# A hybrid decoder block: the two output projections change places, and each head pair's convolution is woven into that pair's own substitution

## The chip, the cores and the metric

One core of one Trainium2 chip. The metric is the device time of one execution in microseconds (us). The chip's engines run side by side, each through its own instructions in a fixed order: TensorE (PE in the profile; PEld are its weight loads), VectorE (DVE), ScalarE (ACT), GpSimd (POOL), and SyncE (SP), which here only issues transfers.

## The reference, cut to what matters

One decoder block on 528 positions (16 learned ones, then 512) of 1024 channels. Two token mixers read the same normalised input `h`, their outputs are projected, gated and added, and a projection, a norm and a gated feed-forward part follow:

```python
p = h @ w_in
y_conv = swish(LN(causal_dwconv31(glu(p)))) @ w_conv_out      # conformer branch
y_rwkv = (LN_head(recurrence(r, decay, k, v, a, b)) + bonus) * g @ w_rwkv_out   # 16 heads of 64
y = sigmoid(gA) * y_conv + sigmoid(gB) * y_rwkv
h = LN(alpha * h + y @ w_o)
h = LN(alpha * h + conv_gated_mlp(h))
```

The recurrence runs over positions, S_t = S_{t-1} diag(w_t) + (S_{t-1} a_t) b_t^T + v_t k_t^T. The kernel solves it in 9 chunks of 64 positions: within a chunk a triangular system is inverted, and the state goes from chunk to chunk.

## The kernel before, in words

Everything lies with channels on the 128 partitions and positions along the free axis. A product of float32 data is made from three products of float32r parts: `wload` (L155) and `wsplit` (L143, with `split`, L136) load a 512 KB block of weights into `wr` (two buffers), round it on ScalarE (`wh`, L138) and take the rest on VectorE (`wl`, L141); `gemm` (L158) then issues 3 x 8 matmuls for a half of the positions (258 or 256 columns). A projection of one 128-channel block is two halves, 48 matmuls.

The 16 heads are done as 8 pairs. The steps of a pair `p`, each one letter in the string `SCHEDULE`:

- `K` (`rkv`, L339): three projections for k, v, r.
- `P` (`prep`, L347): decays (a scan, L383), the arrays `AR`, `BK`, `BT`, `UV`, and the chunk matrices `Gt` (L452). `AR`, `Gt`, `BT`, `UV` have two buffers, so `P` of pair p overwrites what `C` of pair p-2 has read.
- `S` (`solve`, L482): the blocks of `Gt` go through DRAM (`dA`, L493) into a layout `L` (L502), where VectorE inverts all triangles by 31 dependent steps (L520, L524, L526) and, for the short first chunk, 15 more (L530). The result goes to DRAM (`dT`, L544). A second digit names a convolution whose VectorE instructions are put between the dependent steps; the function `behind` fixes that order: each step of the substitution stands behind the instruction taken from the convolution.
- `C` (`merge`, L548, and `chain`, L581): fetches the inverse, combines blocks by matmuls (L566, L571), then goes through the 9 chunks one after the other on TensorE and ScalarE (L584, L603, L606, L620), with a state update on VectorE (L615).
- `F` (`finish`, L624): head norm, the gate by `g_up`, and the store of the pair's output to DRAM (`o_dr`, L673).
- `G` (`glu`, L678): two projections and the gated input of the convolution for block p. `conv` (L701) is the 31-tap convolution of the block, 48 VectorE instructions (L711, L712, L714, L722), stored to `c_dr` (L725).
- `T`: a convolution by itself at lowest priority (`back`). `A`: one of 16 gate projections (`gate`, L728), stored to `g_dr`. `N`: `conv_norm` (L745), the layer norm over the convolution's 1024 channels: sums, subtractions, squares, a reciprocal, then swish, rounding and rest (L755 to L783).

The string gives priorities, not times. The compiler's scheduler keeps one order per engine; instructions traced under `front` go ahead of others, a ready instruction of low priority fills a gap, and the blocks of weights stream through `wr`, `wh`, `wl` in the order of the string. In the kernel before, block 0 and block 5 are convolved by themselves (`T0`, `T5`), and the other blocks are woven into the substitution of the pair before theirs (`S01`, `S12`, `S23`, `S34`, `S56`, `S67`); `S4` and `S7` carry none.

After the string come, in this order, the conformer projection (L811 to L821, weights `w_conv_out`, input `zh`, `zl` from `conv_norm`, result to `ya_dr`), the recurrence's projection (L830 to L855, weights `w_rwkv_out`, input `oh`, `ol`, which are loaded from `o_dr` (L834) and split; it adds `ya` and leaves `yh`, `yl`), and `w_o` with the first layer norm in two halves of positions (L862 to L897). Of the 8 blocks of `w_o`, `NKEEP` = 6 are loaded once and kept for both halves, 2 are loaded for each half. The feed-forward part follows.

SBUF pools are opened on a left and a right stack; a tile of a new pool waits for the tiles that lay at its address. `scan` (left) holds what `P`, `S`, `C`, `F` share, `proj` (right) the rest of them and the convolutions.

Of the kernel before, what the change touches and what calls it, by code (L numbers as in the profile page):

```python
# [11 lines left out]
F32 = mybir.dt.float32  # L12
F32R = mybir.dt.float32r
AF = mybir.ActivationFunctionType
ALU = mybir.AluOpType
# [3 lines left out]
P = 128  # L19
D = 1024  # L20
NK = D // P
# [11 lines left out]
NQ = T - Q0  # L33
# [9 lines left out]
GN_EPS = 64e-5  # L43
EXPM05 = float(np.exp(-0.5))
BACK = 3000
NKEEP = 6
GW = 132


SCHEDULE = ("G0 K0 P0 T0 G1 S01 K1 P1 C0 K2 F0 G2 S12 K3 P2 C1 G3 F1 K4 S23 G4 P3 C2 F2 A S34 K5 P4 C3 F3 G5 S4 A "  # L50
            "T5 K6 P5 G6 C4 F4 S56 P6 C5 K7 F5 G7 S67 A A A P7 C6 F6 S7 A A C7 A A N A A A A A A A F7")


@with_exitstack
def hybrid_block(ctx: ExitStack, tc: tile.TileContext, a, out, dbg=None):
    nc = tc.nc
    V, S, G, TE = nc.vector, nc.scalar, nc.gpsimd, nc.tensor
# [5 lines left out]
    def pool(stack, name, side, **kw):  # L63
        return stack.enter_context(tc.tile_pool(name=name, bufs=1, side=side, reuse_waits="tile", **kw))

    front = tc.high_priority
# [18 lines left out]
    gbank = lambda: bank("g", 3)  # L85
# [50 lines left out]
    def split(dst_hi, dst_lo, src, hi_engine="s"):  # L136
        if hi_engine == "s":
            S.copy(out=dst_hi, in_=src)  # L138
        else:
            V.tensor_copy(out=dst_hi, in_=src)  # L140
        V.tensor_tensor(out=dst_lo, in0=src, in1=dst_hi.bitcast(F32), op=ALU.subtract)  # L141
# [13 lines left out]
    def wload(dram, c0, wpool=None, after=None, bufs=2):  # L155
        return wsplit(dram[:, c0:c0 + P].rearrange("(k p) n -> p k n", p=P), [P, NK, P], wpool, after, bufs)

    def gemm(ps, w, xh, xl, sl, nk=NK):  # L158
        wh, wl = w
        for k in range(nk):  # L160
            TE.matmul(ps, wh[:, k, :], xh(k, sl), start=(k == 0), stop=False)  # L161
            TE.matmul(ps, wl[:, k, :], xh(k, sl), start=False, stop=False)  # L162
            TE.matmul(ps, wh[:, k, :], xl(k, sl), start=False, stop=(k == nk - 1))  # L163
# [59 lines left out]
    with tc.tile_pool(name="start", bufs=1, side="right", reuse_waits="tile") as st:  # L223
        prow = [st.tile([P, P], F32, name=f"prow{i}") for i in range(6)]
        with front():
            xt = []
            for i in range(5):
                n = NMETA if i == 0 else P
# [18 lines left out]
        fw = a["ffn_dw"][0].rearrange("j (c p) -> (j c) p", p=P)  # L247
# [51 lines left out]
        for i, n in ((1, 112), (2, 128), (3, 120), (4, 88), (5, 44)):  # L299
# [15 lines left out]
                    in1=taps[:, :, 1, :], op=ALU.add)  # L315
# [470 lines left out]
    for step in SCHEDULE.split():  # L786
        what, p, q = step[0], int(step[1:2] or 0), int(step[2:] or -1)
        if what == "K":
            raw[p] = rkv(p)
        elif what == "P":  # L790
            prs[p] = prep(p, *raw.pop(p))
        elif what == "S":
            solved[p] = solve(prs[p], conv(q, cpads.pop(q)) if q >= 0 else ())
        elif what == "C":
            with front():
                merge(prs[p], *solved[p])
                ys[p] = chain(prs[p])
        elif what == "F":
            finish(prs[p], ys.pop(p))
        elif what == "G":  # L800
            cpads[p] = glu(p)
        elif what == "T":
            with back():
                for _ in conv(p, cpads.pop(p)):
                    pass
        elif what == "A":
            gate(gates.pop(0))
        elif what == "N":
            ctx_a1.close()
            rb, zh, zl = conv_norm()  # L810
    for j in range(NK):  # L811
        ga = rb.tile([P, NQ], F32, name="ga", bufs=2)
        nc.sync.dma_start(out=ga, in_=g_dr[j])
        w = wload(a["w_conv_out"][0], P * j)
        for sl, n in qsl:
            pt = gbank()
            gemm(pt[:, :n], w, lambda k, s: zh[k][:, s], lambda k, s: zl[k][:, s], sl)
            with front():
                V.scalar_tensor_tensor(out=ga[:, sl], in0=ga[:, sl], scalar=1.0, in1=pt[:, :n],
                                       op0=ALU.add, op1=ALU.mult)  # L820
        nc.sync.dma_start(out=ya_dr[j], in_=ga)  # L821
    ctx_b1.close()
    ctx_a2.close()


    ctx_b2, ctx_o = ExitStack(), ExitStack()
    op = pool(ctx_o, "rout", "left")
    mp = pool(ctx_b2, "mix", "right")
    ot = lambda dt, name: op.tile([P, NQ], dt, name=name, tag="ot", bufs=16)
    yt = lambda dt, name: mp.tile([P, NQ], dt, name=name, tag="yt", bufs=16)  # L830
    oh, ol, yh, yl = [], [], [], []
    for j in range(NK):
        o_t = op.tile([P, NQ], F32, name="o_t", bufs=2)
        nc.sync.dma_start(out=o_t, in_=o_dr[j])  # L834
        oh.append(ot(F32R, "oh"))
        ol.append(ot(F32R, "ol"))
        split(oh[j], ol[j], o_t)
    for j in range(NK):
        gb_ = op.tile([P, NQ], F32, name="gb_", bufs=2)
        nc.sync.dma_start(out=gb_, in_=g_dr[8 + j])  # L840
        ya = op.tile([P, NQ], F32, name="ya", bufs=2)
        nc.sync.dma_start(out=ya, in_=ya_dr[j])
        w = wload(a["w_rwkv_out"][0], P * j)
        yh.append(yt(F32R, "yh"))
        yl.append(yt(F32R, "yl"))
        for sl, n in qsl:
            pt = gbank()
            gemm(pt[:, :n], w, lambda k, s: oh[k][:, s], lambda k, s: ol[k][:, s], sl)
            with front():
                V.scalar_tensor_tensor(out=gb_[:, sl], in0=gb_[:, sl], scalar=1.0, in1=pt[:, :n],  # L850
                                       op0=ALU.add, op1=ALU.mult)
            V.tensor_tensor(out=ya[:, sl], in0=ya[:, sl], in1=gb_[:, sl], op=ALU.add)
            S.activation(out=yh[j][:, sl], in_=ya[:, sl], func=AF.Copy, scale=0.5)
            V.scalar_tensor_tensor(out=yl[j][:, sl], in0=ya[:, sl], scalar=0.5, in1=yh[j][:, sl].bitcast(F32),
                                   op0=ALU.mult, op1=ALU.subtract)  # L855


    ctx_o.close()
    h1h, h1l = hhi[:, :, Q0:T], hlo[:, :, Q0:T]
    ctx_f = ExitStack()  # L860
    fw = pool(ctx_f, "upw", "left")
    kept = [wload(a["w_o"][0], P * j, mp, bufs=NKEEP) for j in range(NKEEP)]  # L862
    half_tile = lambda name, n, bufs: mp.tile([P, 258], F32, name=name, bufs=bufs)[:, :n]
    for (t0, t1), (sl, n) in zip(QH, qsl):
        pm, pv = abank(), abank()
        xs = []
        s1, s2 = half_tile("s1", n, 1), half_tile("s2", n, 1)
        for j in range(NK):
            w = kept[j] if j < NKEEP else wload(a["w_o"][0], P * j)
            pt = gbank()  # L870
            gemm(pt[:, :n], w, lambda k, s: yh[k][:, s], lambda k, s: yl[k][:, s], sl)
            x1 = half_tile("x1", n, 10)
            with front():
                V.scalar_tensor_tensor(out=x1, in0=hlo[:, j, t0:t1].bitcast(F32), scalar=ALPHA,
                                       in1=pt[:, :n], op0=ALU.mult, op1=ALU.add)
                V.scalar_tensor_tensor(out=x1, in0=hhi[:, j, t0:t1].bitcast(F32), scalar=ALPHA,
                                       in1=x1, op0=ALU.mult, op1=ALU.add)
            xs.append(x1)
            if j > 0:
                V.tensor_tensor(out=s1, in0=xs[0] if j == 1 else s1, in1=x1, op=ALU.add)  # L880
        TE.matmul(pm[:, :n], ones_d, s1, start=True, stop=True)
        with front():
            for j in range(NK):
                V.tensor_tensor(out=xs[j], in0=xs[j], in1=pm[:, :n], op=ALU.subtract)
                sq = s2 if j == 0 else half_tile("xsq", n, 2)
                S.activation(out=sq, in_=xs[j], func=AF.Square)
                if j > 0:
                    V.tensor_tensor(out=s2, in0=s2, in1=sq, op=ALU.add)
            TE.matmul(pv[:, :n], ones_d, s2, start=True, stop=True)
            rs1 = mp.tile([P, 258], F32, name="rs1")[:, :n]  # L890
            S.activation(out=rs1, in_=pv[:, :n], func=AF.Sqrt, bias=eps_ln)
            V.reciprocal(out=rs1, in_=rs1)
            for j in range(NK):
                V.tensor_tensor(out=xs[j], in0=xs[j], in1=rs1, op=ALU.mult)
                S.activation(out=xs[j], in_=xs[j], func=AF.Identity, scale=par("ln1_g", j), bias=par("ln1_b", j))
                split(h1h[:, j, sl], h1l[:, j, sl], xs[j], "s")
    dump("h1", h1h.bitcast(F32))  # L897


    fl = ExitStack()  # L900
    ctx_b2.close()
    fp = pool(fl, "ffn", "right")
    hidh = fp.tile([P, NF, SEQ], F32R, name="hidh")
# [113 lines left out]
```

## Time and profile before

| | us |
|---|---|
| runs | 1181.91, 1185.55, 1191.15 (median 1185.55) |
| the profiled execution, its own time | 1188.6 |
| its span | 1186.6 |
| TensorE busy (share of the span) | 1128.4 (95%) |
| VectorE busy | 870.5 (73%) |
| ScalarE busy | 560.5 (47%) |

The profile is one execution. The span is the time from the first to the last instruction that it records; 2.0 us of the execution's own time lie outside. An instruction's line is that of the kernel's file, of a helper's where a helper issues it. "Busy" of TensorE counts matmuls that overlap each other.

### The profile page before, as it was taken

Reading aid. Unit: us, or ns where it says so; the run is one execution under the profiler, and the core shown is the slowest. Engines: PE = TensorE matmul, PEld = TensorE weight load, DVE = VectorE, ACT = ScalarE, POOL = GpSimd, SP = SyncE. Lnnn points to the kernel's source line nnn. Section 1 sums busy time; section 2 is a strip of 40 time slices with the busy share of each in tenths; the row PEclk is TensorE's granted clock in tenths of the full one; section 3 lists DMA queues with packets and bytes.
Section 4 is the critical chain, followed back from the end, with each engine's and each line's share of the span. In section 5 each row is a group of like instructions: output and inputs, shape, how many; then the busy total and the mean of one; then the engine's idle time right before and its main releaser. Section 6 shows DMA issues by size and latency. Waiting matters only on the chain.

```text
span 1186.6 us, 22669 instructions
## 1 busy us (share of the span) xinstructions
PE 1128.4 (95%) x8718; PEld 1062.5 (90%) x8718; DVE 870.5 (73%) x2195; ACT 560.5 (47%) x1195; POOL 85.0 (7%) x242
## 2 busy tenths in 40 slices
PE   4998999999999999999978989999999999999997
PEld 3997989989898989998978989989999999998885
DVE  8598988989899998986495346688876666652227
ACT  3544355647556565666575433346433443432120
POOL 6001011101101110101000000000000000000000
PEclk9999999999999999999898989999999999999999
DMA  5324241333424143344443376523332323343321
GB/s 159 82 80 106 64 117 41 90 82 89 95 60 108 41 104 84 79 121 108 135 125 85 103 209 193 164 58 85 107 100 80 104 75 107 90 134 98 93 85 71
DMA packets 202439, 118.99 MB, mean 100 GB/s; under 512 B 50036, under 2 KB 186397, under 8 KB 202331
## 3 DMA queue, kind: packets, MB, share of 16 engines
q1 hardware_dynamic: 182992, 113.81, 34.1%
q10 hardware_dynamic: 17515, 3.17, 1.5%
q8 instruction: 68, 1.11, 0.4%
q0 software_dynamic: 1824, 0.57, 0.2%
q14 instruction: 40, 0.33, 0.1%
HBM read 102.24 MB, written 15.28 MB: 99 GB/s over the span
## 4 chain that ended last, share of the span: by engine, by line
PE 60%; DVE 8%; DMA 7%; ACT 3%; issue 2%; ACTq 0%; SPq 0%; DVEq 0%; POOL 0%; POOLq 0%
PE ps_g L161 13%; PE ps_g L162 13%; PE ps_g L163 13%; PE ps_x L584 7%; PE psf L961 3%; PE psf L963 3%; PE psf L962 3%; DMA wr<-in_w_o_dram 2%; DMA t22s<-dT 1%; DMA o_t<-o_dr 1%; DVE wl L141 1%; ACT wh L138 1%; PE ps_a L450 1%; DMA wr<-in_ffn_up_dram 1%; PE ps_m L571 1%
## 5 line engine op out<-in xcount | busy, mean ns | idle before, releaser
L161 PE MATMUL ps_g<-hhi,wh 128*128 128x256 f32 (+2 forms) x1648 | 477.2, 290 | 7.9 <-ACT hf_t L277 3.9
L162 PE MATMUL ps_g<-hhi,wl 128*128 128x256 f32 (+2 forms) x1648 | 477.3, 290 | 0.0
L163 PE MATMUL ps_g<-hlo,wh 128*128 128x256 f32 (+2 forms) x1648 | 474.6, 289 | 0.0
L161 PEld LDWEIGHTS ps_g<-hhi,wh 128*128 128x128 f32 x1648 | 312.8, 190 | 11.3 <-ACT hf_t L277 4.5
L162 PEld LDWEIGHTS ps_g<-hhi,wl 128*128 128x128 f32 x1648 | 312.4, 190 | 2.6 <-issue 0.6
L163 PEld LDWEIGHTS ps_g<-hlo,wh 128*128 128x128 f32 x1648 | 312.9, 190 | 1.3 <-issue 0.4
L141 DVE TENSOR_TENSOR wl<-wr,wh 128x1024 fp32r<-128x1024 f32 x151 | 184.1, 1220 | 96.6 <-ACT wh L138 96.0
L138 ACT CAST wh<-wr 128x1024 fp32r<-128x1024 f32 x151 | 158.0, 1047 | 124.8 <-PE psf L962 75.2
L722 DVE SCALAR_TENSOR_TENSOR cev<-cd,drv,cev 128x257 f32<-128x257 f32 x216 | 99.1, 478 | 0.1
L919 ACT COPY pu<-ps_g 128x258 f32<-128x258 f32 (+1 forms) x88 | 32.8, 373 | 111.1 <-PE ps_g L163 111.0
L584 PE MATMUL ps_x<-UV,Gt 128*66 128x64 f32 (+1 forms) x576 | 71.3, 246 | 4.2 <-DMA Gt<-dT 3.8
L584 PEld LDWEIGHTS ps_x<-UV,Gt 128*66 128x66 f32 (+1 forms) x576 | 65.5, 168 | 6.1 <-DMA Gt<-dT 4.0
L961 PE MATMUL psf<-wh,hidh 128*128 128x512 f32 x176 | 69.3, 394 | 0.0
L963 PE MATMUL psf<-wl,hidh 128*128 128x512 f32 x176 | 69.0, 392 | 0.0
L962 PE MATMUL psf<-wh,hidl 128*128 128x512 f32 x176 | 68.3, 388 | 0.0
L926 DVE SCALAR_TENSOR_TENSOR u<-pu,prm,u 128x512 f32<-128x512 f32 x88 | 65.7, 748 | 1.3
L714 DVE SCALAR_TENSOR_TENSOR csh<-cpad,drv,csh 128x257 f32<-128x257 f32 x120 | 57.5, 479 | 0.5
L615 DVE SCALAR_TENSOR_TENSOR Sb<-Sb,lc,ps_x 64x64 f32<-64x64 f32 x112 | 31.3, 280 | 32.7 <-PE ps_x L584 31.2
L924 DVE TENSOR_SCALAR u<-pu,prm 128x512 f32<-128x512 f32 x44 | 21.2, 485 | 43.5 <-ACT pu L919 43.4
L524 DVE TENSOR_TENSOR stmp<-L,W 128x60 f32<-128x60 f32 (+21 forms) x216 | 45.3, 210 | 1.3
L526 DVE TENSOR_TENSOR W<-W,stmp 128x60 f32<-128x60 f32 (+21 forms) x216 | 45.2, 209 | 1.0
L161 PE MATMUL ps_g<-zh,wh 128*128 128x258 f32 (+1 forms) x128 | 38.5, 303 | 7.6 <-ACT zh L138 7.6
(308 smaller groups left out, 1991.9 us busy)
## 6 DMA issues: line engine op xcount, KB each, us to landing
wr<-in_w_in_dram SPq DMA_DIRECT2D x59, 512.0 KB, 4.3
wr<-in_ffn_up_dram SPq DMA_DIRECT2D x44, 512.0 KB, 4.0
wr<-in_ffn_down_dram SPq DMA_DIRECT2D x22, 512.0 KB, 3.7
wr<-in_w_o_dram SPq DMA_DIRECT2D x10, 512.0 KB, 4.9
g_dr<-gt SPq DMA_DIRECT2D x16, 257.0 KB, 3.0
L<-dA SPq DMA_DIRECT2D x32, 128.0 KB, 4.2
wr<-in_w_conv_out_dram SPq DMA_DIRECT2D x8, 512.0 KB, 4.4
wr<-in_w_rwkv_out_dram SPq DMA_DIRECT2D x8, 512.0 KB, 5.6
```

The costliest lines, as they stand in the source:

```text
L138: S.copy(out=dst_hi, in_=src)
L141: V.tensor_tensor(out=dst_lo, in0=src, in1=dst_hi.bitcast(F32), op=ALU.subtract)
L161: TE.matmul(ps, wh[:, k, :], xh(k, sl), start=(k == 0), stop=False)
L162: TE.matmul(ps, wl[:, k, :], xh(k, sl), start=False, stop=False)
L163: TE.matmul(ps, wh[:, k, :], xl(k, sl), start=False, stop=(k == nk - 1))
L584: mm = lambda o, l, r, start: TE.matmul(o, l, r, start=start, stop=True, skip_group_check=True)
L714: yield V.scalar_tensor_tensor(out=cs_, in0=x1[:, i:i + NM], scalar=dcol(D_SCW, 8 * i + j) if i < HT else dcol(D_HCW, 8 * 2 * i + j), in1= ...
L722: yield V.scalar_tensor_tensor(out=yp[:, b, :] if lasttap else ev[:, b, :], in0=d[:, i:i + NM], scalar=dcol(D_HCW, 8 * (2 * i + b) + j), i ...
L926: V.scalar_tensor_tensor(out=u, in0=p_[:, t:t + SEQ], scalar=pcol(C_FW, 44 * t + m), in1=u, op0=ALU.mult, op1=ALU.add)
L961: TE.matmul(acc[t][d], hidh[:, k, ts], wd[k][0][:, ds], start=(k == 0), stop=False)
L962: TE.matmul(acc[t][d], hidl[:, k, ts], wd[k][0][:, ds], start=False, stop=False)
L963: TE.matmul(acc[t][d], hidh[:, k, ts], wd[k][1][:, ds], start=False, stop=(k == NF - 1))
```

## The change

The two projections change places. The outputs of the pairs are loaded, all eight into buffers of their own, and projected first; that result times its gate goes to `ya_dr`. `conv_norm` is traced after that projection and no longer has a letter in the string. The conformer's projection comes second, reads `ya` back, adds, and leaves `yh`, `yl`. Each convolution is woven into the substitution of its own pair (`S00`, `S11`, to `S77`); no `T` is left. The string places the gate projections anew: of 16, one each stands before `K5`, `K6` and `S66`, 2 before `S77`, 1 before `C7`, 7 before `F7` and 3 behind it. `NKEEP` is 4, so 4 blocks of `w_o` are loaded for each half. The pool `mix` moves to the left stack, and the small tiles of the first layer norm get a pool `norm1` on the right.

```diff
-NKEEP = 6
+NKEEP = 4
-SCHEDULE = ("G0 K0 P0 T0 G1 S01 K1 P1 C0 K2 F0 G2 S12 K3 P2 C1 G3 F1 K4 S23 G4 P3 C2 F2 A S34 K5 P4 C3 F3 G5 S4 A "
-            "T5 K6 P5 G6 C4 F4 S56 P6 C5 K7 F5 G7 S67 A A A P7 C6 F6 S7 A A C7 A A N A A A A A A A F7")
+SCHEDULE = ("G0 K0 P0 S00 K1 G1 P1 C0 K2 F0 S11 K3 P2 C1 G2 F1 K4 S22 P3 C2 G3 F2 A K5 S33 P4 C3 G4 F3 A K6 S44 P5 C4 "
+            "G5 F4 K7 S55 P6 C5 G6 F5 A S66 P7 C6 G7 F6 A A S77 A C7 A A A A A A A F7 A A A")
...
-        elif what == "N":
-            ctx_a1.close()
-            rb, zh, zl = conv_norm()
+
+    ctx_a2.close()
+    ctx_o = ExitStack()
+    op = pool(ctx_o, "rout", "left")
+    ot = lambda dt, name: op.tile([P, NQ], dt, name=name, tag="ot", bufs=16)
+    oh, ol = [], []
     for j in range(NK):
+        o_t = op.tile([P, NQ], F32, name="o_t", bufs=NK)
+        nc.sync.dma_start(out=o_t, in_=o_dr[j])
+        oh.append(ot(F32R, "oh"))
+        ol.append(ot(F32R, "ol"))
+        split(oh[j], ol[j], o_t)
+    for j in range(NK):
+        gb_ = op.tile([P, NQ], F32, name="gb_", bufs=2)
+        nc.sync.dma_start(out=gb_, in_=g_dr[8 + j])
+        w = wload(a["w_rwkv_out"][0], P * j)
+        for sl, n in qsl:
+            pt = gbank()
+            gemm(pt[:, :n], w, lambda k, s: oh[k][:, s], lambda k, s: ol[k][:, s], sl)
+            with front():
+                V.scalar_tensor_tensor(out=gb_[:, sl], in0=gb_[:, sl], scalar=1.0, in1=pt[:, :n],
+                                       op0=ALU.add, op1=ALU.mult)
+        nc.sync.dma_start(out=ya_dr[j], in_=gb_)
+    ctx_a1.close()
+    rb, zh, zl = conv_norm()
+    ctx_o.close()
+    ctx_f, ctx_b2 = ExitStack(), ExitStack()
+    fw = pool(ctx_f, "upw", "left")
+    mp = pool(ctx_b2, "mix", "left")
...
+        ya = mp.tile([P, NQ], F32, name="ya", bufs=2)
+        nc.sync.dma_start(out=ya, in_=ya_dr[j])
         w = wload(a["w_conv_out"][0], P * j)
+        yh.append(yt(F32R, "yh"))
+        yl.append(yt(F32R, "yl"))
         for sl, n in qsl:
             pt = gbank()
             gemm(pt[:, :n], w, lambda k, s: zh[k][:, s], lambda k, s: zl[k][:, s], sl)
...
-        nc.sync.dma_start(out=ya_dr[j], in_=ga)
...
-            V.tensor_tensor(out=ya[:, sl], in0=ya[:, sl], in1=gb_[:, sl], op=ALU.add)
+            V.tensor_tensor(out=ya[:, sl], in0=ya[:, sl], in1=ga[:, sl], op=ALU.add)
             S.activation(out=yh[j][:, sl], in_=ya[:, sl], func=AF.Copy, scale=0.5)
...
+    ctx_n = ExitStack()
+    lnp = pool(ctx_n, "norm1", "right")
     kept = [wload(a["w_o"][0], P * j, mp, bufs=NKEEP) for j in range(NKEEP)]
-    half_tile = lambda name, n, bufs: mp.tile([P, 258], F32, name=name, bufs=bufs)[:, :n]
+    half_tile = lambda name, n, bufs: lnp.tile([P, 258], F32, name=name, bufs=bufs)[:, :n]
```

## Rows read from the trace of the kernel before

**Rows 1.** The page's part 1: busy us, share of the span, instructions.
```profile
PE 1128.4 (95%) x8718; PEld 1062.5 (90%) x8718; DVE 870.5 (73%) x2195; ACT 560.5 (47%) x1195; POOL 85.0 (7%) x242
```

**Rows 2.** Busy time by stretch: length, PE (matmuls), PEld, DVE, ACT, POOL, clock, DMA, GB/s.
```profile
560.00:580.00 20.00, 18.05 (x135) 16.46 (x134) 8.09 (x28) 11.51 (x33) 2.05 (x4) 0.83 0.28 57
...
600.00:620.00 20.00, 15.78 (x126) 14.73 (x125) 19.17 (x56) 17.49 (x37) 1.72 (x2) 0.99 0.39 121
620.00:640.00 20.00, 13.61 (x84) 13.11 (x85) 15.05 (x37) 12.07 (x21) 0.00 (x0) 0.67 0.19 37
...
680.00:700.00 20.00, 16.99 (x135) 16.16 (x134) 8.34 (x13) 6.06 (x8) 0.00 (x0) 0.96 0.88 250
700.00:720.00 20.00, 19.56 (x141) 19.11 (x141) 11.08 (x24) 7.03 (x12) 0.00 (x0) 0.87 0.58 180
...
820.00:840.00 20.00, 20.00 (x172) 20.00 (x171) 17.59 (x25) 11.94 (x19) 0.00 (x0) 1.00 0.38 107
```

**Rows 3.** Waits of PE: line, releaser, us in total, times, longest.
```profile
PE ps_g L161 <- ACT zh L138: 7.6, 1, 7.6
...
PE ps_g L161 <- ACT oh L138: 2.9, 3, 1.5
```

**Rows 4.** Busy time by stretch, three longer ones (columns as in rows 2).
```profile
160.00:500.00 340.00, 334.00 (x2749) 310.32 (x2749) 306.34 (x1000) 202.99 (x509) 44.24 (x119) 0.99 0.34 81
540.00:600.00 60.00, 57.89 (x466) 53.89 (x465) 34.26 (x124) 35.62 (x91) 5.56 (x15) 0.94 0.51 133
...
588.00:631.00 43.00, 32.26 (x243) 30.29 (x243) 41.24 (x125) 31.88 (x63) 1.72 (x2) 0.87 0.34 111
```

**Rows 5.** By stretch, L722 alone (31 per convolution), then tile W alone: DVE busy.
```profile
0.00:161.00 161.00, 28.58 (x62) 0.99 0.36 101
...
437.00:501.00 64.00, 16.78 (x37) 1.00 0.38 89
...
588.00:632.00 44.00, 12.59 (x58) 0.00 (x0) 0.86 0.34 108
```

**Rows 6.** Timeline of SP's queue: start, us, issued transfers.
```profile
437.31 1.25 SPq L544 DMA_DIRECT2D dT<-W  x2
...
501.36 1.21 SPq L544 DMA_DIRECT2D dT<-W  x2
...
547.64 1.21 SPq L544 DMA_DIRECT2D dT<-W  x2
...
631.18 1.21 SPq L544 DMA_DIRECT2D dT<-W  x2
...
677.75 0.38 SPq L673 DMA_DIRECT2D o_dr<-on  x1
...
700.32 2.57 SPq L834 DMA_DIRECT2D o_t<-o_dr  x2
```

**Rows 7.** Timeline of ACT, the last chunk of pair 7.
```profile
667.10 0.26 ACT L620 COPY Y<-ps_x 64x128 f32<-64x128 f32 x1 [0.75 <-PE ps_x L584]
```

**Rows 8.** Groups of DVE: busy us, mean ns of one, idle before them.
```profile
L141 DVE TENSOR_TENSOR wl<-wr,wh 128x1024 fp32r<-128x1024 f32 x151 | 184.1, 1220 | 96.6 <-ACT wh L138 96.0
L722 DVE SCALAR_TENSOR_TENSOR cev<-cd,drv,cev 128x257 f32<-128x257 f32 x216 | 99.1, 478 | 0.1
...
L714 DVE SCALAR_TENSOR_TENSOR csh<-cpad,drv,csh 128x257 f32<-128x257 f32 x120 | 57.5, 479 | 0.5
```

**Rows 9.** Tiles on, o_t (landing), oh, gt: ns min/median/max of one, first and last start.
```profile
DMA to landing us min/median/max: 3.0/3.0/3.6
...
DMA to landing us min/median/max: 3.9/5.1/6.2
...
L161 PE MATMUL ps_g<-oh,wh x128: 277/282/583, 693.7 to 747.1; 128*128 128x258 f32 x64, 128*128 128x256 f32 x64
...
L736 ACT ACTIVATE gt<-ps_g,drv x32: 461/476/480, 276.0 to 614.7; 128x258 f32<-128x258 f32 x16, 128x256 f32<-128x256 f32 x16
```

**Rows 10.** The page's part 6: transfers of w_o, KB each, us to landing.
```profile
wr<-in_w_o_dram SPq DMA_DIRECT2D x10, 512.0 KB, 4.9
```

More of the change, by code (lines that the diff above doesn't have):

```diff
@@ L807, in hybrid_block @@
             gate(gates.pop(0))
-        elif what == "N":
-            ctx_a1.close()
-            rb, zh, zl = conv_norm()
-    for j in range(NK):
[L812 to L820, printed above, removed]
-        nc.sync.dma_start(out=ya_dr[j], in_=ga)
[L822 to L833, printed above, removed]
+    ctx_a2.close()
[3 more added lines that the diff above has]
+    oh, ol = [], []
+    for j in range(NK):
+        o_t = op.tile([P, NQ], F32, name="o_t", bufs=NK)
         nc.sync.dma_start(out=o_t, in_=o_dr[j])
@@ L840, in hybrid_block @@
         nc.sync.dma_start(out=gb_, in_=g_dr[8 + j])
-        ya = op.tile([P, NQ], F32, name="ya", bufs=2)
-        nc.sync.dma_start(out=ya, in_=ya_dr[j])
         w = wload(a["w_rwkv_out"][0], P * j)
-        yh.append(yt(F32R, "yh"))
-        yl.append(yt(F32R, "yl"))
         for sl, n in qsl:
@@ L851, in hybrid_block @@
                                        op0=ALU.add, op1=ALU.mult)
-            V.tensor_tensor(out=ya[:, sl], in0=ya[:, sl], in1=gb_[:, sl], op=ALU.add)
+        nc.sync.dma_start(out=ya_dr[j], in_=gb_)
[5 more added lines that the diff above has]
+    mp = pool(ctx_b2, "mix", "left")
+    yt = lambda dt, name: mp.tile([P, NQ], dt, name=name, tag="yt", bufs=16)
+    yh, yl = [], []
+    for j in range(NK):
+        ga = mp.tile([P, NQ], F32, name="ga", bufs=2)
+        nc.sync.dma_start(out=ga, in_=g_dr[j])
+        ya = mp.tile([P, NQ], F32, name="ya", bufs=2)
+        nc.sync.dma_start(out=ya, in_=ya_dr[j])
+        w = wload(a["w_conv_out"][0], P * j)
+        yh.append(yt(F32R, "yh"))
+        yl.append(yt(F32R, "yl"))
+        for sl, n in qsl:
+            pt = gbank()
+            gemm(pt[:, :n], w, lambda k, s: zh[k][:, s], lambda k, s: zl[k][:, s], sl)
+            with front():
+                V.scalar_tensor_tensor(out=ga[:, sl], in0=ga[:, sl], scalar=1.0, in1=pt[:, :n],
+                                       op0=ALU.add, op1=ALU.mult)
+            V.tensor_tensor(out=ya[:, sl], in0=ya[:, sl], in1=ga[:, sl], op=ALU.add)
             S.activation(out=yh[j][:, sl], in_=ya[:, sl], func=AF.Copy, scale=0.5)
@@ L855, in hybrid_block @@
                                    op0=ALU.mult, op1=ALU.subtract)
-    ctx_o.close()
+    ctx_b1.close()
     h1h, h1l = hhi[:, :, Q0:T], hlo[:, :, Q0:T]
-    ctx_f = ExitStack()
-    fw = pool(ctx_f, "upw", "left")
+    ctx_n = ExitStack()
+    lnp = pool(ctx_n, "norm1", "right")
     kept = [wload(a["w_o"][0], P * j, mp, bufs=NKEEP) for j in range(NKEEP)]
-    half_tile = lambda name, n, bufs: mp.tile([P, 258], F32, name=name, bufs=bufs)[:, :n]
+    half_tile = lambda name, n, bufs: lnp.tile([P, 258], F32, name=name, bufs=bufs)[:, :n]
     for (t0, t1), (sl, n) in zip(QH, qsl):
@@ L889, in hybrid_block @@
             TE.matmul(pv[:, :n], ones_d, s2, start=True, stop=True)
-            rs1 = mp.tile([P, 258], F32, name="rs1")[:, :n]
+            rs1 = lnp.tile([P, 258], F32, name="rs1")[:, :n]
             S.activation(out=rs1, in_=pv[:, :n], func=AF.Sqrt, bias=eps_ln)
@@ L900, in hybrid_block @@
     fl = ExitStack()
+    ctx_n.close()
     ctx_b2.close()
```

## The prediction

> **What bounds the kernel now.** I read the page's busy shares first, then busy time by stretch, then the waits of TensorE, then the queue of transfers for the times at which each pair's steps end. TensorE is busy 1128.4 of 1186.6 us [rows 1], so it bounds nearly everything, and what a change can win lies in the few stretches where it is not dense. The reader is to compare the counts of matmuls: a dense stretch of 20 us holds 172 (the last of [rows 2]). The five sparse ones around the end of the head pairs hold 135, 126, 84, 135 and 141 [rows 2], short of dense by 37 + 46 + 88 + 37 + 31 = 239 matmuls; at 20/172 = 0.1163 us each that is 27.8 us. The waits say why. Near 620 TensorE stands 7.6 us for the first `zh`, that is for the norm over the convolutions, and near 690 for `oh`, the outputs of the pairs [rows 3]. In both places the clock drops (granted 0.67 and 0.87 of full speed on average, so part of the stretch ran at 1.2 instead of 2.4 GHz after TensorE had stood idle) [rows 2].
>
> By busy time the same five stretches lack only 2.0 + 4.2 + 6.4 + 3.0 + 0.4 = 16.0 us. The Trainium skill (page "Perfetto Trace Analysis", section "Identifying the Most-Contended Engine") says that matmul busy time is a bad measure, since pipelined instructions hide gaps, and that weight-load busy time is better. By that the stretches lack 3.5 + 5.3 + 6.9 + 3.8 + 0.9 = 20.4 us, and the change could win 20 and not 16; the trace goes further still, to 27.8 by the count. I use the count.
>
> VectorE is the second bound, inside the pairs: from 160 to 500 it is busy 306.3 of 340 us (90%) [rows 4]. From 540 to 600 it has only 34.3 of 60, and from 588 to 631 it is full again, 41.2 of 43 [rows 4]: there the substitution of pair 7 (58 instructions, 12.6 us [rows 5]) shares the engine with the norm over the convolutions. It ends at 631.2 [rows 6], 84 us after pair 6 (547.6), where the pairs before took 46 (501.4 to 547.6) and 64 (437.3 to 501.4) [rows 6]. The 16 gate projections, the filler of the pairs, are over at 614.7 [rows 9].
>
> **Part 1: the projections change places.** The matmuls are the same, two times 8 x 48 = 384, or 44.7 us dense each. What changes is what must be ready. Before, the conformer's projection needs the norm and lies beside chain and finish of pair 7; the recurrence's comes last. Now the recurrence's comes first and needs pair 7's output, and after it nothing is late: the norm over the convolutions lies beside those 44.7 us. It was 41.2 - 12.6 = 28.6 us of VectorE at most [rows 4, 5]; if this cover were gone it would be seen whole. So everything hangs on X, the time at which the recurrence's projection can start. The second projection then ends at X + 89.4; before, it ended at about 747.5 (its last group of matmuls starts at 747.1 [rows 9]). Even is X = 658.1.
>
> X follows from the time S7 at which pair 7 is solved. Before: solved at 631.2, last chunk 667.1 [rows 7], store of the output 677.75 [rows 6]; so 35.9 and 10.6 us. Then the store lands in 3.0 us and the load in 5.1 us (3.9 to 6.2) [rows 9], rounding and rest take an estimated 1.3 (half of the 1.22 for a tile twice as wide [rows 8], on each of two engines), and TensorE can do 7 of 8 parts of the first half, 21 matmuls or 2.4 us, ahead of it. Together X = S7 + 35.9 + 10.6 + 7.0 = S7 + 53.5. Even is S7 = 604.6. The other seven outputs have buffers of their own now and can be fetched earlier; before, with two, the loads stretched to 700.3 and later [rows 6]. Should they still wait for each other, the 54 us that this projection took before (693.7 to 747.5 [rows 9]) instead of 44.7 are the bound, 9 us more.
>
> **Part 2: each convolution in its own pair.** A convolution is 31 instructions of 478 ns and 15 of 479 ns [rows 8], 22 us of VectorE. Before, two are done by 161 (62 of L722), and between 437 and 501 another 37 of those instructions run, more than one convolution [rows 5]: the engine is one to two convolutions ahead. Now pair p is to carry only its own. If VectorE alone bounds the pairs, pair 5 is solved up to 1.5 x 22 = 33 us earlier than 501.4; if the latency of transfers and chunks does, 0. VectorE is 90% busy [rows 4], so I lean to the first and take 20: pair 5 at 481. Pairs 6 and 7 each have a convolution of their own now: between 46 and 64 us per pair [rows 6], I take 55.5. That gives S7 = 592. From below, VectorE's work: 631.2 less the 28.6 that the norm took, less at most 25.7 idle from 540 to 600 [rows 4], is 577. From above: pair 7's substitution starts at 588 as now and the convolution's 22 us stand where the norm's stood, S7 = 588 + 12.6 + 22 and some 6 of splits, 628. I keep 577 to 628 for the range.
>
> With the edges that `behind` adds, a late convolution holds the whole substitution, and behind that stand on VectorE the splits of weights (1.22 us each [rows 8]) on which TensorE waits. The cover is that the input of convolution 7 is made well ahead; if not, it is the slow case below.
>
> With S7 = 592, X = 645.5 and the second projection ends at 734.9 in place of 747.5: 12.6 us won.
>
> **Part 3: the gates, moved.** They are the same 16 x 48 matmuls at the same price; they only fill. Their fresh place in the string matters if TensorE has none left at the end. Work alone sets X at 658.1 - 27.8 = 630 at the earliest, so at X = 645 TensorE has some 15 us thin, and the clock may drop there as it does now between 620 and 640 [rows 2]. I charge 2 us, between 0 and the 31 matmuls, 3.6 us, that the stretch from 700 lacks.
>
> **Part 4: two blocks of `w_o` more.** `NKEEP` 4 loads 12 blocks instead of 10. Each costs a transfer of 4.9 us [rows 10], a rounding and a rest of 1.22 us [rows 8]. All hidden: 0; all exposed, with about 1.1 for the rounding: 14.4. Transfers and splits lie beside matmuls of the second half, 24 per block or 2.8 us, so I take 1.5. They stand ahead of the first `ffn_up` blocks in SP's queue and in `wr`; that is what would pay. The buffers of the second projection's gate lie where `oh` lay, so its first load (5.1 us as for `o_t`) starts late; three result banks of 24 matmuls, 8.4 us, cover it. Moved pools cost nothing else that I see.
>
> **Sum.** -12.6 + 2 + 1.5 = -9.1 us. The profiled execution took 1188.6 (span 1186.6 and 2.0 around it) and would take 1179.5; it stands 3.05 above the median of the runs, 1185.55, so the median becomes 1176.4.
>
> **Rivals.**
> Full cover: S7 near 577 and fillers to the end, so that TensorE stays dense and all 27.8 us come back: 1185.55 - 27.8 + 1.5 = 1159.3. For it: the idle VectorE from 540 to 600. Against it: 35.9 us of chunks and 18 of finish, transfers and splits follow S7 whatever the fillers do.
>
> Slower: pair 7 becomes the bound. S7 = 628, X = 681.5, the second projection ends at 770.9, 23.4 late, plus 2 and 1.5: 1212.4. It decides from S7 = 613 on (slower by over 1%); between 598 and 613 it eats the win. For it: pair 7 has no convolution before and gets one; the projection that used to fill TensorE beside its chunks is moved behind them. Against it: the 25.7 us that VectorE has idle before 600 take the convolution.
>
> The weave does not do what it says: the scheduler already ran convolutions ahead of where the string puts them [rows 5], and may again, so that S7 stays near 602 and the end where it was: about 1186.
>
> **How the numbers follow.** About 1%, 11.9 us, is what a measurement of this kernel can tell from no change. The forecast (S7 from 584 to 598, 1168 to 1182) has 0.45, full cover 0.20, the weave that changes nothing 0.17, pair 7 as bound 0.18. Faster by over 1% (under 1173.7) are full cover, the forecast's lower third, 0.16, and a little of the third case: 0.38. Slower by over 1% is nearly all of the last: 0.17. The rest, 0.45, is within 1%. The range leaves out half of either end: 1159 to 1206.
>
> **What would show it.** Right: the norm's VectorE work beside the recurrence's projection and no wait for `zh`; pair 0 solved some 20 us sooner than before, pair 7 near 592; the recurrence's projection starting near 645 after a short wait for pair 7's `oh`; both projections dense at about 172 matmuls per 20 us; the stretch from 620 to 645 thin. Wrong: pair 7 solved after 605, a long wait for `oh` with the clock low and no gates left, or a new wait for `wh` in the second half of `w_o`.

## The result, and the profile after

The changed kernel takes 1201.55 us (median of 4 runs, 1194.79 to 1203.81) against 1186.79 of the kernel before on the same chip: a ratio of 1.0121, 95% interval 1.0084 to 1.0157. It is slower by 1.2%, and the forecast was 9 us faster. The profiled execution took 1203.81 us; its span is 1202.1, so 15.5 us longer than that of before.

The page's part 1 of the kernel after:

```profile
PE 1137.4 (95%) x8718; PEld 1073.6 (89%) x8718; DVE 877.6 (73%) x2197; ACT 564.2 (47%) x1199; POOL 85.1 (7%) x242
```

The same 8718 matmuls are "busy" 9.0 us longer than in [rows 1]: some of them ran at the lower clock. Where, the stretches tell (columns as in [rows 2]):

```profile
540.00:600.00 60.00, 60.00 (x516) 57.03 (x517) 46.81 (x163) 34.31 (x87) 4.21 (x12) 1.00 0.54 148
600.00:620.00 20.00, 15.22 (x87) 12.79 (x86) 11.11 (x31) 10.80 (x28) 0.00 (x0) 0.70 0.29 73
620.00:640.00 20.00, 16.99 (x80) 14.55 (x79) 11.41 (x23) 6.41 (x18) 0.00 (x0) 0.50 0.00 0
640.00:660.00 20.00, 5.78 (x19) 3.85 (x18) 10.53 (x25) 18.99 (x35) 0.00 (x0) 0.50 0.21 54
660.00:680.00 20.00, 19.84 (x142) 19.54 (x143) 9.99 (x16) 6.45 (x9) 0.00 (x0) 0.85 0.54 180
680.00:700.00 20.00, 20.00 (x169) 20.00 (x168) 7.70 (x11) 4.21 (x4) 0.00 (x0) 1.00 0.60 189
...
780.00:800.00 20.00, 15.20 (x120) 14.71 (x119) 17.44 (x41) 10.95 (x22) 0.00 (x0) 0.98 0.20 58
800.00:820.00 20.00, 19.16 (x147) 18.82 (x147) 17.07 (x36) 9.84 (x19) 0.00 (x0) 0.94 0.44 128
820.00:840.00 20.00, 16.19 (x109) 15.73 (x109) 14.13 (x30) 11.76 (x27) 0.00 (x0) 0.83 0.09 28
```

Two things have changed places. From 540 to 600 TensorE is now dense (516 matmuls where [rows 4] had 466). From 600 to 660 it is nearly empty: 87 + 80 + 19 = 186 matmuls where three dense stretches hold 3 x 172 = 516, at a granted clock of 0.50, that is at 1.2 GHz, for most of it. Read the row of 620 to 640 with care: "17 of 20 us busy" is 80 matmuls of 172, since a matmul at half clock is busy about twice as long (up to 582 ns against a median of 282 in the row of `oh` below). The Trainium skill (page "Perfetto Trace Analysis", section "Identifying the Most-Contended Engine") prefers weight-load busy time, and the share of peak arithmetic, to matmul busy time, because pipelined instructions "look smaller in the trace". The trace agrees in part: weight loads are busy 14.55 of 20 us, which is nearer to the count, but still far from it. A second thin stretch, from 780 to 840, is `w_o` and the norm behind it; in [rows 2] the last third of it is dense.

The queue of transfers gives the milestones of pair 7 (as [rows 6]):

```profile
545.71 1.22 SPq L544 DMA_DIRECT2D dT<-W  x2
...
595.01 1.62 SPq L544 DMA_DIRECT2D dT<-W  x2
...
654.75 0.33 SPq L673 DMA_DIRECT2D o_dr<-on  x1
655.13 4.04 SPq L816 DMA_DIRECT2D o_t<-o_dr  x8
```

Pair 7 is solved at 595.0, 36 us earlier than before and 3 later than forecast. Its output is stored 59.7 us after that, where before it was 677.75 - 631.18 = 46.6. All eight outputs are fetched together behind this store; none was fetched earlier. The tiles on TensorE and the gates (as [rows 9]):

```profile
L736 ACT ACTIVATE gt<-ps_g,drv x32: 461/477/498, 264.1 to 603.4; 128x258 f32<-128x258 f32 x16, 128x256 f32<-128x256 f32 x16
...
L161 PE MATMUL ps_g<-oh,wh x128: 278/282/582, 659.8 to 708.9; 128*128 128x258 f32 x64, 128*128 128x256 f32 x64
...
L161 PE MATMUL ps_g<-zh,wh x128: 277/283/290, 709.2 to 755.1; 128*128 128x258 f32 x64, 128*128 128x256 f32 x64
...
L161 PE MATMUL ps_g<-yh,wh x128: 278/282/550, 755.5 to 809.2; 128*128 128x258 f32 x64, 128*128 128x256 f32 x64
```

The last gate is out at 603.4, so nothing is left to run beside pair 7. The recurrence's projection starts at 659.8, the conformer's follows without a gap, and `w_o` starts at 755.5, where it was 747.4: 8.1 us of the 15.5 are lost by then. The other 7.4 come in and after `w_o`, which now loads 12 blocks (group of the page's part 6, as [rows 10]):

```profile
wr<-in_w_o_dram SPq DMA_DIRECT2D x12, 512.0 KB, 5.0
```

Last, the waits of TensorE (as [rows 3]) and one chunk of pair 7's chain on ScalarE. The wait for `zh`, 7.6 us, is gone; in its place stand waits for pair 7's `oh` and along pair 7's finish and chain:

```profile
PE ps_x L646 <- ACT Y L642: 7.5, 5, 6.7
...
PE ps_g L161 <- ACT oh L138: 5.6, 1, 5.6
...
PE ps_x L584 <- ACT Rz L603: 4.3, 9, 1.1
...
PE ps_x L584 <- ACT UV L606: 3.7, 7, 1.6
```

The chunk in the kernel before (timeline of ScalarE: start, us, and in brackets the idle time ahead of it), then in the kernel after:

```profile
654.53 0.26 ACT L620 COPY Y<-ps_x 64x128 f32<-64x128 f32 x1 [0.97 <-PE ps_x L584]
655.59 0.26 ACT L603 COPY Rz<-ps_x 64x128 f32<-64x128 f32 x1 [0.80 <-PE ps_x L584]
656.39 0.26 ACT L606 COPY UV<-ps_x 64x128 f32<-64x128 f32 x1 [0.54 <-PE ps_x L584]
657.62 0.26 ACT L620 COPY Y<-ps_x 64x128 f32<-64x128 f32 x1 [0.97 <-PE ps_x L584]
```

```profile
620.28 0.26 ACT L620 COPY Y<-ps_x 64x128 f32<-64x128 f32 x1 [1.63 <-PE ps_x L584]
621.48 0.26 ACT L603 COPY Rz<-ps_x 64x128 f32<-64x128 f32 x1 [0.94 <-PE ps_x L584]
622.55 0.26 ACT L606 COPY UV<-ps_x 64x128 f32<-64x128 f32 x1 [0.80 <-PE ps_x L584]
624.43 0.26 ACT L620 COPY Y<-ps_x 64x128 f32<-64x128 f32 x1 [1.63 <-PE ps_x L584]
...
637.86 0.26 ACT L620 COPY Y<-ps_x 64x128 f32<-64x128 f32 x1 [1.63 <-PE ps_x L584]
...
639.36 1.28 ACT L778 ACT_TABLE_LOAD   x1
...
642.82 0.26 ACT L620 COPY Y<-ps_x 64x128 f32<-64x128 f32 x1 [0.68 <-PE ps_x L584]
```

The first chunk behind the merge ends with this copy, before and after:

```profile
644.72 0.26 ACT L620 COPY Y<-ps_x 64x128 f32<-64x128 f32 x1 [0.97 <-PE ps_x L584]
```

```profile
611.82 0.26 ACT L620 COPY Y<-ps_x 64x128 f32<-64x128 f32 x1 [0.97 <-PE ps_x L584]
```

The copies last the same 0.26 us. What grew is the time for which ScalarE waits for the small matmuls: 0.97 + 0.80 + 0.54 = 2.31 before, 1.63 + 0.94 + 0.80 = 3.37 after. A chunk takes 4.15 us (624.43 - 620.28) instead of 3.09. The last chunk takes 4.96, because the norm's swish has to load its table on ScalarE in the middle of it.

### The profile page after: what moved, and what is told of

It is laid out like the page before. It is cut to its first block, busy times and chain, and to the rows that moved or that the text cites. A ratio compares the mean times of both kernels' runs of the same rounds, so it can differ in the third digit from the quotient of the medians.

```text
span 1202.1 us, 22660 instructions
## 1 busy us (share of the span) xinstructions
PE 1137.4 (95%) x8718; PEld 1073.6 (89%) x8718; DVE 877.6 (73%) x2197; ACT 564.2 (47%) x1199; POOL 85.1 (7%) x242
## 4 chain that ended last, share of the span: by engine, by line
PE 65%; DVE 8%; DMA 3%; ACT 3%; issue 1%; ACTq 0%; POOL 0%; SPq 0%; DVEq 0%; POOLq 0%
PE ps_g L161 15%; PE ps_g L162 15%; PE ps_g L163 15%; PE ps_x L584 8%; PE psf L968 3%; PE psf L970 3%; PE psf L969 3%; DVE wl L141 1%; PE ps_a L450 1%; DMA wr<-in_ffn_up_dram 1%; DVE csh L714 1%; DVE cev L722 1%; ACT wh L138 1%; PE ps_m L566 1%; PE ps_m L571 1%
## 5 line engine op out<-in xcount | busy, mean ns | idle before, releaser
L722 DVE SCALAR_TENSOR_TENSOR cev<-cd,drv,cev 128x257 f32<-128x257 f32 x216 | 98.0, 479 | 0.2
L584 PE MATMUL ps_x<-UV,Gt 128*66 128x64 f32 (+1 forms) x576 | 75.9, 257 | 4.8 <-DMA Gt<-dT 2.3
L584 PEld LDWEIGHTS ps_x<-UV,Gt 128*66 128x66 f32 (+1 forms) x576 | 70.8, 179 | 6.7 <-DMA Gt<-dT 2.5
L161 PE MATMUL ps_g<-oh,wh 128*128 128x258 f32 (+1 forms) x128 | 37.5, 293 | 5.6 <-ACT oh L138 5.6
```

The costliest lines, as they stand in the source:

```text
L584: mm = lambda o, l, r, start: TE.matmul(o, l, r, start=start, stop=True, skip_group_check=True)
L722: yield V.scalar_tensor_tensor(out=yp[:, b, :] if lasttap else ev[:, b, :], in0=d[:, i:i + NM], scalar=dcol(D_HCW, 8 * (2 * i + b) + j), i ...
```

## The experiments

Theory A, which most expectations are built on: each convolution in its own pair wins time; the order of the projections loses more, because chain and finish of pair 7 then have TensorE for themselves, partly at 1.2 GHz; the two further blocks of `w_o` cost some us more. What the rivals are stands in the expectations. Each kernel is compared with the kernel before on its own chip (1185.09 us for e1, e3, e4 and e5, 1186.34 for e6 to e9), and ratios carry 95% intervals.

**e1: the kernel before with `NKEEP` = 4, nothing else.**

```diff
-NKEEP = 6
+NKEEP = 4
```

> The kernel before with NKEEP 4 in place of 6, nothing else. Theory A (the two further blocks of w_o for each half push the first blocks of ffn_up back and cost the 7 us that the changed kernel lost after the start of w_o): 6 to 9 us over the kernel before, about 1194. Theory B (these 7 us come from the moved pools or from the later start, not from the blocks): within 2 us of the kernel before.

1190.92 us, ratio 1.0045 (1.0019 to 1.0071): 5.8 us more, between 2 and 8, just under the 6 to 9 of theory A. Up to `w_o` it stands as before (first `w_o` matmul at 748.7, before 747.4); from there to the first `ffn_down` matmul it takes 1064.7 - 748.7 = 316.0 us, before 1057.3 - 747.4 = 309.9. So two blocks cost about 6 us, not the 1.5 of the forecast, and they are most of the 7.4 us that the changed kernel loses after `w_o` begins. The other profiles agree: from the first `w_o` matmul to the end of the span, the three kernels with `NKEEP` 6 (before, e4, e7) take 437.6 to 439.6 us, the seven with 4 take 443.3 to 446.8.

**e4: the weave alone.** The kernel before with the new string (an `N` behind `C7`, which the old order needs), old order of projections, `NKEEP` 6. "Weave" stands here and below for the whole string; it also places the gates anew, and no run separates the two.

```diff
...
-            "T5 K6 P5 G6 C4 F4 S56 P6 C5 K7 F5 G7 S67 A A A P7 C6 F6 S7 A A C7 A A N A A A A A A A F7")
...
+            "G5 F4 K7 S55 P6 C5 G6 F5 A S66 P7 C6 G7 F6 A A S77 A C7 N A A A A A A A F7 A A A")
```

> The kernel before with the changed string alone (each convolution in its own pair, gates as in the change, the norm over the convolutions traced behind C7), the conformer's projection still first, NKEEP 6. Theory A (the weave brings pair 7 forward, and only the order of the projections loses): pair 7 solved near 595 in place of 631, its chain beside gates and projection at about 36 us, total 10 to 30 us under the kernel before, 1157 to 1177. Theory B (the weave itself is what costs): 1187 or more.

1168.32 us, ratio 0.9841 (0.9803 to 0.9879): the best kernel of this study, faster than both. Theory A held for the total; pair 7 was solved at 608.7, though, not near 595. The weave by itself wins 17 to 19 us.

**e5: the order alone.** The changed kernel with the string of before (without its `N`).

```diff
...
-            "G5 F4 K7 S55 P6 C5 G6 F5 A S66 P7 C6 G7 F6 A A S77 A C7 A A A A A A A F7 A A A")
...
+            "T5 K6 P5 G6 C4 F4 S56 P6 C5 K7 F5 G7 S67 A A A P7 C6 F6 S7 A A C7 A A A A A A A A A F7")
```

> The changed kernel with the string of the kernel before (without its N): the recurrence's projection first, convolutions woven as before. Theory A (the weave helps, the order costs): pair 7 solved later than 595, total over the changed kernel, 1205 to 1225. Theory B (the weave costs, the order helps): pair 7 solved earlier, total under 1195.

1214.18 us, ratio 1.0229 (1.0195 to 1.0263), as theory A had it. Pair 7 is solved at 611.4, stored at 666.8, `w_o` starts at 767.6. Against e1, which differs by the order (with the pools that go with it), this is 1214.18 - 1190.92 = 23 us; against the changed kernel, which differs by the weave, 13 us more.

**e9: the weave with `NKEEP` 4, old order** (e4 with the one line of e1). Its projections are in the old order; besides that, only the pools and buffers that go with the order differ from the changed kernel.

> The changed string with the conformer's projection first, as in e4, but NKEEP 4. With it the changed kernel differs from this one in the order of the projections alone. Theory A (weave, order and NKEEP add up): e4 plus the 5.8 us of e1, about 1174, and the order alone costs 1201.5 - 1174 = 27 us. Theory B (the three depend on each other): under 1170 or over 1180.

1172.23 us, ratio 0.9892 (0.9867 to 0.9917). Theory A held (about 1174, and 27 us for the order). `NKEEP` costs 3.9 us here by the medians, 6 by the ratios, whose intervals overlap a little; the order alone costs 1201.55 - 1172.23 = 29 us (27 by the two ratios). Tiles on TensorE of e9, then two of its stretches and its milestones on the queue of transfers:

```profile
L161 PE MATMUL ps_g<-oh,wh x128: 278/282/290, 678.9 to 725.7; 128*128 128x258 f32 x64, 128*128 128x256 f32 x64
...
L161 PE MATMUL ps_g<-zh,wh x128: 277/282/584, 616.9 to 678.5; 128*128 128x258 f32 x64, 128*128 128x256 f32 x64
...
L161 PE MATMUL ps_g<-yh,wh x128: 278/283/356, 726.1 to 775.8; 128*128 128x258 f32 x64, 128*128 128x256 f32 x64
```

```profile
600.00:620.00 20.00, 8.94 (x51) 7.50 (x49) 15.48 (x26) 12.52 (x24) 1.54 (x2) 0.66 0.25 59
620.00:640.00 20.00, 20.00 (x183) 19.25 (x182) 10.24 (x28) 11.59 (x30) 0.00 (x0) 1.00 0.17 54
640.00:660.00 20.00, 20.00 (x165) 19.43 (x165) 9.43 (x23) 10.34 (x21) 0.00 (x0) 1.00 0.52 147
```

```profile
605.02 1.38 SPq L544 DMA_DIRECT2D dT<-W  x2
...
654.56 0.32 SPq L673 DMA_DIRECT2D o_dr<-on  x1
```

This pair of kernels is the clearest of all. From 600 to 620 e9 is thin too, but dense from there on. Pair 7 is solved 10 us later in e9 (605.0 and 595.0), yet its output is stored at the same moment, 654.6 and 654.8. And while e9 was doing that, TensorE was dense at full clock with the conformer's projection. When the changed kernel starts its first projection at 659.8, e9 has evicted 9 of the 16 halves of its own; 9 x 24 matmuls at 0.1163 us are 25.1 us. With the 4.7 us that the changed kernel's first projection takes beyond 44.7 (most of it while the clock is at half, until 666.1) that makes 29.8, about the 29.4 us by which `w_o` starts later, 755.5 against 726.1.

**e3: only the clock.** The changed kernel, with 12 further matmuls per chunk of pair 7's chain that nothing reads, so that TensorE has work beside it.

```diff
+        wt = mbank() if pr["p"] == 7 else None
+
+        def warm():
+            for _ in range(4 if wt is not None else 0):
+                TE.matmul(wt[:, 0:256], hhi[:, 0, 0:P], hhi[:, 1, 0:256], start=True, stop=True)
...
             S.copy(out=R[0:64, :], in_=X[0:64, 0:P])
+            warm()
...
             S.copy(out=UV[0:64, c, :], in_=X[0:64, P:2 * P])
+            warm()
...
             S.copy(out=yo, in_=X[64:128, 0:P])
+            warm()
```

> The changed kernel, with 12 matmuls of 128x256 in each of the 9 chunks of pair 7's chain that nobody reads; they keep TensorE occupied and nothing else. Theory A (the last chain is slow because TensorE has nothing else and its clock is granted at half): pair 7 from solved to last chunk falls from 47.8 to about 36 us, the recurrence's projection from 49 to 45, and the total is 14 to 17 us under the changed kernel, about 1186. Theory B (the chain waits for ScalarE's copies and for VectorE, the clock does not matter): it stays at 47 us or grows, and the total stays at 1201 or above.

1200.37 us, ratio 1.0126 (1.0084 to 1.0167): no gain that can be told from none, so theory A's total (about 1186) was wrong here. From solved to last chunk pair 7 took 41.1 us, not about 36, and the projection 48.2, not 45. Theory A's mechanism was seen in the chunks all the same:

```profile
600.00:620.00 20.00, 17.24 (x149) 16.04 (x148) 13.02 (x34) 10.97 (x30) 0.90 (x2) 1.00 0.38 94
620.00:640.00 20.00, 16.70 (x147) 15.51 (x145) 8.15 (x20) 7.71 (x21) 0.00 (x0) 0.96 0.01 1
640.00:660.00 20.00, 5.93 (x19) 4.14 (x20) 13.12 (x29) 18.90 (x35) 0.00 (x0) 0.50 0.30 90
```

```profile
614.24 0.26 ACT L628 COPY Y<-ps_x 64x128 f32<-64x128 f32 x1
...
637.82 0.26 ACT L628 COPY Y<-ps_x 64x128 f32<-64x128 f32 x1 [0.75 <-PE ps_x L584]
```

The clock is at or near full beside the chunks, and from the first of them after the merge to the last they take 637.8 - 614.2 = 23.6 us; in the changed kernel 642.8 - 611.8 = 31.0, in the kernel before 667.1 - 644.7 = 22.4. So keeping the clock up gives back 7.4 us of chain. From 640 to 660, in the finish, the clock is at half again. But the finish then took 652.87 - 637.8 = 15.1 us instead of 11.9: the norm's swish, with its table loads, fell into it on ScalarE, and the output was stored only 1.9 us earlier.

**e6: e3, and the norm's swish held behind the rounding of pair 7's output on ScalarE.**

```diff
...
+            sw = S.activation(out=cs[j], in_=cs[j], func=AF.Silu, scale=par("conv_ln_g", j), bias=par("conv_ln_b", j))
+            behind(sw, o_split[0], "swish behind the outputs")
...
```

> e3 (changed kernel with matmuls nobody reads in pair 7's chain) in which the swish of the norm over the convolutions stands behind the rounding of pair 7's output on ScalarE. Theory A (in e3 the 5 us won in the chain were lost because ScalarE did the norm's swish, rounding and table loads among pair 7's finish): the finish shortens, the recurrence's projection starts 4 to 7 us sooner than the 658.5 of e3, total about 1194. Theory B (the finish is a chain of its own latencies): no change, about 1200.

1198.81 us, ratio 1.0113 (1.006 to 1.0166). The finish is 11.2 us now, the first projection starts at 653.6 instead of 658.5, as theory A had it, and `w_o` at 749.8. The total missed the 1194 of theory A: the time can't be told from that of the changed kernel (2.7 us less by the medians, the intervals overlap). The chunks are near the price of before (638.2 - 614.6 = 23.6 us) and the finish is undisturbed, yet the kernel is still 1.1% slower than before. Of the 29.4 us by which `w_o` starts later than in e9, this run takes back 5.7 (755.5 - 749.8), and 2.2 of these lie in pair 7 being solved earlier. So what the low clock and the disturbed finish cost is the smaller part of the loss.

**e8: gates as the filler.** The changed kernel with the last five gate projections held behind chunks of pair 7's chain.

```diff
...
+            x = 2 * (j - 11) + i
+            gemm(pt[:, :n], w, hh, hl, slice(t0, t1), after=last_chain[min(x, 8)] if x >= 0 else None)
```

> The changed kernel with the last 5 of the 16 gate projections held behind the chunks of pair 7's chain on TensorE (order alone, no work added). Theory A (the chain lacked a filler at full clock): its chunks fall from 4.35 to about 3.2 us, the recurrence's projection runs dense, and the total falls by 8 to 14 us to about 1190. Theory B (TensorE has nothing else to do wherever the gates stand, the hole only moves to pair 6): pair 7 is solved no earlier than 595, the total stays within 4 us of 1201.5.

1215.31 us, ratio 1.0263 (1.0234 to 1.0292): with e5 the slowest of all, and 14 us over the changed kernel, where theory B had at most 4.

```profile
560.00:580.00 20.00, 16.30 (x78) 13.94 (x78) 6.09 (x26) 3.64 (x15) 0.00 (x0) 0.50 0.55 165
580.00:600.00 20.00, 14.13 (x56) 10.44 (x55) 15.66 (x61) 9.75 (x26) 0.00 (x0) 0.50 0.00 0
...
640.00:660.00 20.00, 20.00 (x171) 19.07 (x169) 6.10 (x20) 12.67 (x29) 0.00 (x0) 1.00 0.21 60
```

Most of the chain of pair 7 is covered now (640 to 660 is dense), and the hole has moved to pair 6: 78 and 56 matmuls where the changed kernel has 181 and 170, at half clock from 559 to 607, and pair 7 is solved at 611.1 instead of 595.0. The gates are as much needed there. In this placing there isn't filler enough for both; other placings were not tried.

**e7: e4 with the norm traced under `front`,** so that the conformer's projection can start sooner.

```diff
-            rb, zh, zl = conv_norm()
+            with front():
+                rb, zh, zl = conv_norm()
```

> e4 (changed string, conformer's projection first, NKEEP 6) with the norm over the convolutions given high priority, so that it goes ahead of pair 7's substitution on VectorE. If the wait for zh is what is left there: the conformer's projection starts some 8 us sooner than the 620 of e4 and covers pair 7's chain, total about 1160. If pair 7 is what is left: it is solved later than 609, total 1168 or more.

1177.93 us, ratio 0.9935 (0.9911 to 0.996). The projection starts at 608.4 instead of 620.2, but pair 7 is solved 19 us later (628.1 instead of 608.7): between 599 and 618 VectorE did the norm and only a few steps of the substitution. It is 9.6 us worse than e4 by the medians: with the weave in place, the later pair 7 costs more than the earlier projection gives.

All in one table, from the profiles (us; "tail" is from solved to stored, "rest" from stored to the first matmul of `w_o`):

| kernel | order | weave | pair 7 solved | stored | tail | rest | `w_o` starts |
|---|---|---|---|---|---|---|---|
| before | old | old | 631.2 | 677.8 | 46.6 | 69.6 | 747.4 |
| e1 | old | old | 633.2 | 680.3 | 47.1 | 68.4 | 748.7 |
| e4 | old | own | 608.7 | 658.6 | 49.9 | 72.0 | 730.6 |
| e9 | old | own | 605.0 | 654.6 | 49.5 | 71.5 | 726.1 |
| e7 | old, norm first | own | 628.1 | 677.6 | 49.5 | 61.0 | 738.6 |
| after | new | own | 595.0 | 654.8 | 59.7 | 100.7 | 755.5 |
| e3 | new | own | 596.7 | 652.9 | 56.2 | 100.1 | 753.0 |
| e6 | new | own | 592.8 | 649.4 | 56.6 | 100.4 | 749.8 |
| e8 | new | own | 611.1 | 664.7 | 53.5 | 104.0 | 768.7 |
| e5 | new | old | 611.4 | 666.8 | 55.4 | 100.8 | 767.6 |

"Rest" is the order's own price: 100 to 104 us where both projections stand behind pair 7, 61 to 72 where all of the recurrence's and only the end of the conformer's do. "Tail" is what the prediction took for unchanged.

## Why the prediction was wrong, step by step

**Pair 7 solved at 592 (Part 2): right in the number, and in part by luck.** It came at 595.0. Pair 5 is solved at 482.2 (forecast 481), pair 0 at 152.8 instead of 160.8 (forecast: some 20 us sooner; it was 8). That VectorE alone bounds the pairs is not shown: it would have made pair 5 up to 33 us earlier, and 19 came. The weave is what it says: 31 instructions of L722, one convolution, run up to 153 and 31 more up to 212.5, where [rows 5] had 62 by 161. Pairs 6 and 7 take 63.5 and 49.3 us, on average 56.4 (forecast 55.5). But the weave is only a part of this gain: with the old order (e4, e9) pair 7 is solved at 608.7 and 605.0, and with the old weave the new order alone takes it from 633.2 (e1) to 611.4 (e5). The new order frees VectorE of most of the norm while pair 7 is solved: the norm's subtractions (L764) start at 603.8, behind the 595.0, and in e9 at 583.9, ahead of the 605.0. Part 2 counted this only in its lower bound.

**Nothing is late after the recurrence's projection (Part 1): right.** `zh` follows `oh` without a wait (708.9 and 709.2) and the second projection is dense; the norm is hidden.

**"35.9 and 10.6 us" from solved to stored (Part 1): the step that failed.** The prediction read these durations off the kernel before, in which a projection lay beside them, and applied them to a kernel in which that projection had just been moved away. They became 47.8 and 11.9. Of the 13.2 us that the way from solved to stored grew by, 3.3 are the way to the first chunk behind the merge (16.8 instead of 13.5; e9 and e4, in the old order, have 16.8 and 17.1, so this is not the order's, and its cause stays open), 8.6 the chunks (31.0 instead of 22.4; e3 takes 7.4 of them back by keeping the clock up), 1.3 the finish, in which ScalarE also does the norm. That the matmuls which had lain beside this way now stand behind it was in the prediction's sum, as X + 89.4; that the way itself grows without them was not.

**Part 3, 2 us for the clock, between 0 and 3.6: mis-sized.** The text saw that TensorE would be thin before X and that the clock may drop, but priced this by a stretch in which a dense projection ran at a low clock for a few us. It was at 1.2 GHz for 58 us (608.0 to 666.1), on the path: 7.4 us of chunks by e3, and the larger part of the 49.4 - 44.7 = 4.7 us by which the first projection ran over (27 matmuls in the 6.3 us up to 666.1, where 0.1163 us each would be 3.1).

**Part 1, 44.7 us for a dense projection: a little mis-sized.** At full clock the matmuls of both projections follow each other at 0.12 us (360 in 43.1 us, 387 in 46.3), not at 0.1163; for 768 matmuls that is some 3 us.

**Part 4, 1.5 us for two blocks: mis-sized.** 5.8 by e1 (2 to 8), 3.9 to 6 by e9 against e4; inside the bounds of 0 to 14.4.

The sum again, in profiled us, forecast and measured:

| term | forecast | measured | difference |
|---|---|---|---|
| pair 7 solved | 592 | 595.0 | +3.0 |
| solved to stored | 46.5 | 59.7 | +13.2 |
| stored to first projection | 7.0 | 5.0 | -2.0 |
| two projections | 89.4 | 95.7 | +6.3 |
| clock, charged apart | 2 | in the rows above | -2.0 |
| `w_o` and on, more than before | 1.5 | 7.4 | +5.9 |

That is 24.4, and with the 0.1 us between 747.5 and 747.4 the way from -9.1 to +15.5 within rounding. X came at 659.8, only 1.7 us past the prediction's even point of 658.1; the other 13.7 of the 15.5 us are the 6.3 of the projections and the 7.4 from `w_o` on.

**The rivals.** The slower one named the right mechanism ("the projection that used to fill TensorE beside its chunks is moved behind them") and hung it on the wrong condition, a pair 7 solved after 613. It came at 595. That the weave changes nothing fell with the 595.0. Full cover did not come: 600 to 660 lay nearly empty, and e8 moved that hole without filling it. What the prediction did not ask is what each part does by itself. It booked the 39 us by which it put pair 7 earlier (36 were measured) against the whole change and found the sum good; in fact the weave wins 17 to 19 us in the old order and 13 in the new, and the order costs 23 to 29.

That the 29 us are the lost cover is shown by e9 beside the changed kernel, as far as the pools that move with the order cost nothing; no run moves these alone. The gain from fetching seven outputs earlier, which the prediction took for possible, did not appear: the eight loads are issued together at 655.1. Whether they could come earlier was not tried.

## What to carry to other kernels

A duration on a serial chain belongs to what ran beside it: before a filler is moved away, price the chain again without it, with the clock at the lower of its two levels and with whatever will be let in on its other engines. Ask of two changes in one what each does alone; here the one was worth -17 us and the other +29 (the rest is `NKEEP`). When two large blocks of matmuls follow a serial tail and only one of them needs it, the other one belongs beside the tail, as in e4 and e9, even if its own input has to be waited for.

## What was not expected of the hardware

Before TensorE's clock fell at 608, its matmuls had thinned out (32 from 601 to 608); it then stayed at 1.2 GHz for 58 us, into the first projection, although pair 7's chain gave it small matmuls for more than half of that time: from 620 to 640 it held 80 of them, "busy" for 17.0 us, at a granted clock of 0.50. In e3 147 matmuls in the same stretch were "busy" for 16.7 us, at a clock of 0.96. The two busy times are alike because a matmul at half clock is busy for longer; only the counts and the clock beside them tell the stretches apart.

On the tail of pair 7 ScalarE goes to and fro between the norm (L773), its swish (L778) and the head norm (L638), and at each change stands an `ACT_TABLE_LOAD` of 1.28 us; the changed kernel has four there (627.0, 639.4, 645.9, 653.0), e9 has two (610.5, 644.0). The Trainium skill (page "ScalarE: Activation LUTs", section "What ACT_TABLE_LOAD costs") gives 1283 ns for the load and about 1380 ns for a drain with it. The trace agrees with the first, and shows no room for the second: the load at 627.00 starts where the copy ahead of it ends (626.72 + 0.26), and the next activation starts at 628.29.
